# The first norm and modulation of a hybrid decoder block, rewritten: other products on TensorE, a quartered root, four differences on GpSimd

## The chip, the cores and the metric

The kernel runs on one core of a Trainium2 chip. The metric is the device time of one execution in microseconds (us). A kernel's time here is the median of several runs. Beside the timed runs, one execution was recorded by the hardware profiler; its span (first to last instruction) is a little shorter than its device time.

The engines are named as the profile names them: PE (TensorE, matrix products; PEld is its loading of the stationary operand), DVE (VectorE), ACT (ScalarE), POOL (GpSimd), SP (SyncE, which issues most transfers here).

## What is computed

One layer of a decoder block for 512 tokens of width 1024, all in float32. The part that matters here is the first line of it: the norm over each token, scaled and shifted by a vector that is computed from the condition `c`.

```python
mod = silu(c) @ ada_w + ada_b                       # 1024 x 6144
shift1, scale1, gate1, shift2, scale2, gate2 = split(mod, 6)
h = rmsnorm(x, norm1_g) * (1 + scale1) + shift1     # x: 512 x 1024
q, k, v, cb, cc, cu = split(h @ w_in, ...)          # 1024 x 2304
...                                                 # attention, short conv, output projection
x = x + gate1 * (merged @ w_out)
h2 = rmsnorm(x, norm2_g) * (1 + scale2) + shift2
x = x + gate2 * peer(h2, ...)                       # product-key experts, nearly all of the time
```

## The kernel before, in words

The activations lie transposed: `xT` holds the 1024 channels as 8 chunks of 128 partitions by 512 tokens. Matrix products that must keep float32's accuracy are made from two parts: `hi` is the operand rounded by ACT (`split`, L176), `lo` is what was cut off, a difference made by DVE (L177), and `mm3` (L200 to L202) adds three products of them in one accumulator.

The first stage goes so. ACT squares the 8 chunks of `xT` (L221), DVE adds them up one after the other (L223), and one product with a matrix of ones (`ss`, L253) sums over the partitions and puts the same sum on all of them, for 512 tokens. ACT takes the root (L241), DVE the reciprocal (L242), both over 128x512. In the meantime `silu(c)` is spread to all partitions as `cact` (`rows_of`, L156 to L160: DVE builds diagonal blocks `dg`, two products with ones turn them into rows).

Then the 8 chunks of `h` are made in the order 5, 6, 7, 0 to 4 (`ORDER`). The shift and scale of a chunk come from `ada_w` in one of two ways. For the chunks 5 to 7 (`NR` = 3), PE multiplies a broadcast column of `silu(c)` with 256 columns of `ada_w` (`ada_rows`, L272, eight products a chunk), which leaves shift and scale as rows on all partitions, and DVE picks the diagonal (`pick`, L290). For the other five, DVE multiplies a transposed 128x1024 block with `cact` and sums it up (`junk`, L213), once for the shift and once for the scale. After that `h` takes four operations a chunk: `f` = x times 1/rms (DVE, L295), scaled and shifted in place (ACT, L296), `hH` (ACT, L176) and `hL` (DVE, L177).

Four blocks of `w_in` (`FIRST`: 4, 5, 0, 1) are loaded between them and split into `hi` and `lo`; as each chunk of `h` is ready, PE runs the 12 products of that chunk into four accumulators `pj`. Weights, `ada_w` blocks and `dg` share five buffers (`LD` = 5, tag `ld`), so SP can issue a transfer only when the user of the buffer five places earlier is done.

Behind this come the angles for the rotary embedding (DVE L313 to L326, ACT `sinT` L324 and `cosT` L327), the norms and rotations of q and k (`q0`, `qk1`, `qk2`: ACT L353 and L355, PE `ssq` L357 and `rot` L368, DVE L363 to L372), and further blocks of `w_in` (`PLAN`: P2, P3 and so on). Each engine has one queue and works it off in order. A scheduler sets that order before the run, from costs of its own; it is fixed in the program.

## Time and profile before

| | us |
|---|---|
| median of 3 timed runs | 1447.48 (1445.46 to 1451.26) |
| the profiled execution, device time | 1445.51 |
| its span | 1443.6 |

How to read it: every row of the profile has a start or a count, a duration, the engine, the line (L177 is line 177 of the kernel before), the operation, `out<-in` by the program's names, and the shape. A product of two float32 operands stands as two MATMUL rows, one for each of its passes (four products of 128x2 are eight rows). Rows of one kind that follow each other are merged, with their count.

### The profile page before, as it was taken

How to read it: one execution, taken by the hardware profiler on the slowest of the kernel's cores; microseconds unless marked ns; L12 is line 12 of the kernel's file. 1: busy time of each engine (PE TensorE's matmuls, PEld its weight loads, DVE VectorE, ACT ScalarE, POOL GpSimd, SP SyncE). 2: the span in 40 equal slices, each digit the busy share in tenths (PEclk: the TensorE clock that was granted, in tenths of full speed). 3: DMA queues.
4: the chain of work that ended last, by engine and by line, in shares of the span. 5: the costliest groups of instructions: out<-in, count | busy, mean ns of one | idle time of the engine just before them, and what ended most of it. 6: DMA issues, size and time to landing. Idle time of an engine off the chain costs nothing.

```text
span 1443.6 us, 21238 instructions
## 1 busy us (share of the span) xinstructions
PE 1391.7 (96%) x7696; PEld 1222.1 (85%) x7696; DVE 1242.0 (86%) x2267; ACT 616.1 (43%) x1041; POOL 411.4 (29%) x292
## 2 busy tenths in 40 slices
PE   6999998999897999999999999999999999999998
PEld 4776776788897999999888888889999999889997
DVE  7778978799989999998668888888789988898964
ACT  4534646423633555464433434343343324333431
POOL 0000000000032330511034444446545546565400
PEclk9999999999998999999999999999999999999999
DMA  8645535222496997898999999999999999999843
GB/s 282 226 164 166 202 124 188 82 85 89 151 305 200 382 377 280 327 384 325 364 332 362 409 395 378 396 357 380 355 362 394 388 357 343 363 343 393 319 146 131
DMA packets 134377, 418.80 MB, mean 290 GB/s; under 512 B 12801, under 2 KB 39553, under 8 KB 132737
## 3 DMA queue, kind: packets, MB, share of 16 engines
q1 hardware_dynamic: 92800, 266.45, 51.1%
q0 software_dynamic: 41472, 151.01, 27.7%
q8 instruction: 60, 0.98, 0.3%
q14 instruction: 45, 0.36, 0.1%
HBM read 375.77 MB, written 41.62 MB: 289 GB/s over the span
## 4 chain that ended last, share of the span: by engine, by line
PE 63%; DVE 24%; DMA 5%; issue 5%; ACT 2%; POOL 1%; SPq 0%; DVEq 0%; ACTq 0%; POOLq 0%
PE o L997 11%; PE o L996 11%; PE o L998 11%; PE pa L200 6%; PE pa L202 6%; PE pa L201 6%; DVE lo L177 4%; DVE junk L213 2%; DVE B L946 2%; DVE junk L784 1%; PE py L200 1%; PE py L201 1%; DVE I L636 1%; PE py L202 1%; POOL row L776 1%
## 5 line engine op out<-in xcount | busy, mean ns | idle before, releaser
L176 ACT ACTIVATE hi<-raw 128x1024 fp32r<-128x1024 f32 x298 | 312.2, 1054 | 308.2 <-PE pa L201 71.7
L177 DVE TENSOR_TENSOR lo<-raw,hi 128x1024 fp32r<-128x1024 f32 x298 | 363.2, 1221 | 42.4 <-ACT hi L176 42.0
L202 PE MATMUL pa<-h2H,lo 128*128 128x352 f32 x1024 | 330.5, 323 | 8.2 <-DVE lo L177 8.2
L200 PE MATMUL pa<-h2H,hi 128*128 128x352 f32 x1024 | 332.9, 325 | 1.4 <-ACT sp L624 1.4
L201 PE MATMUL pa<-h2L,hi 128*128 128x352 f32 x1024 | 329.5, 322 | 0.0
L997 PE MATMUL o<-lo,wwh 128*128 128x512 f32 x768 | 299.2, 390 | 0.9 <-DVE lo L177 0.9
L996 PE MATMUL o<-hi,wwh 128*128 128x512 f32 x768 | 299.6, 390 | 0.0
L998 PE MATMUL o<-hi,wwl 128*128 128x512 f32 x768 | 298.8, 389 | 0.0
L776 POOL DMA_INDIRECT row<-in_uR,eG x128 | 187.4, 1464 | 319.5 <-PE o L998 181.8
L776 POOL DMA_INDIRECT row<-in_vL,eG x128 | 179.8, 1405 | 135.4 <-PE o L998 68.6
L784 DVE SCALAR_TENSOR_TENSOR junk<-row,h2N 128x1024 bf16<-128x1024 f32 x128 | 154.2, 1224 | 63.0 <-DMA row<-in_uR,eG 62.8
L202 PEld LDWEIGHTS pa<-h2H,lo 128*128 128x128 f32 x1024 | 193.2, 189 | 9.4 <-DVE lo L177 9.4
L200 PEld LDWEIGHTS pa<-h2H,hi 128*128 128x128 f32 x1024 | 192.7, 188 | 3.7 <-ACT sp L624 1.5
L201 PEld LDWEIGHTS pa<-h2L,hi 128*128 128x128 f32 x1024 | 193.1, 189 | 2.2
L912 DVE SCALAR_TENSOR_TENSOR ga<-row,av,ga 128x1024 f32<-128x1024 f32 x127 | 163.1, 1284 | 29.7 <-DMA row<-in_vL,eG 22.0
L776 POOL DMA_INDIRECT row<-in_uR,eH x32 | 44.0, 1376 | 493.2 <-DVE eq L695 402.9
L998 PEld LDWEIGHTS o<-hi,wwl 128*128 128x128 f32 x768 | 144.2, 188 | 30.3
L997 PEld LDWEIGHTS o<-lo,wwh 128*128 128x128 f32 x768 | 144.2, 188 | 29.3 <-DVE lo L177 1.5
L996 PEld LDWEIGHTS o<-hi,wwh 128*128 128x128 f32 x768 | 144.1, 188 | 28.3 <-issue 0.2
L176 ACT ACTIVATE wwh<-w 128x768 fp32r<-128x768 f32 x64 | 54.2, 846 | 164.0 <-DVE w L979 118.0
L978 ACT ACTIVATE w<-G 128x32 f32<-128x32 f32 x128 | 22.3, 221 | 190.4 <-DVE wwl L177 179.9
L177 DVE TENSOR_TENSOR wwl<-w,wwh 128x768 fp32r<-128x768 f32 x64 | 61.1, 955 | 9.8 <-ACT wwh L176 9.8
(265 smaller groups left out, 1852.0 us busy)
## 6 DMA issues: line engine op xcount, KB each, us to landing
raw<-in_uL SPq DMA_DIRECT2D x128, 512.0 KB
raw<-in_vL SPq DMA_DIRECT2D x128, 512.0 KB
Gd<-st SPq DMA_DIRECT2D x12, 2048.0 KB
G<-Gd SPq DMA_DIRECT2D x16, 1536.0 KB
ada<-in_ada SPq DMA_DIRECT2D x32, 512.0 KB
Ad<-sp SPq DMA_DIRECT2D x34, 352.0 KB
sp<-Ad SPq DMA_DIRECT2D x34, 352.0 KB
raw<-in_w_in SPq DMA_DIRECT2D x18, 512.0 KB
```

The source lines that it names most:

```text
L176: nc.scalar.activation(h, f, AF.Copy)
L177: nc.vector.tensor_sub(l, f, h.bitcast(F32))
L200: nc.tensor.matmul(ps, wh(k), rh(k), start=(k == k0), stop=False)
L201: nc.tensor.matmul(ps, wh(k), rl(k), start=False, stop=False)
L202: mark[0] = nc.tensor.matmul(ps, wl(k), rh(k), start=False, stop=(k == k1))
L213: nc.vector.scalar_tensor_tensor(junk, raw, 1.0, cact, op0=OP.mult, op1=OP.mult, accum_out=mod[:, b:b + 1])
L776: d = nc.gpsimd.indirect_dma_start(out=t, out_offset=None, in_=tab, in_offset=bass.IndirectOffsetOnAxis(ap=e, axis=0))
L784: return nc.vector.scalar_tensor_tensor(junk, t, 1.0, h, op0=OP.mult, op1=OP.mult, accum_out=a)
L912: nc.vector.scalar_tensor_tensor(ga, t, av[:, k:k + 1], ga, op0=OP.mult, op1=OP.add)
L996: nc.tensor.matmul(o, wh[:, cs], vh[:, hs], start=(j == 0), stop=False)
L997: nc.tensor.matmul(o, wh[:, cs], vl[:, hs], start=False, stop=False)
L998: last = nc.tensor.matmul(o, wl[:, cs], vh[:, hs], start=False, stop=(j == NJ - 1))
```

## The change

It rewrites the first stage and leaves the rest of the kernel's text alone.

- `silu(c)` as rows: eight products of a broadcast column with the identity take the place of the diagonal blocks on DVE. `rows_of` is used once more near the end of the kernel, for `gate2`.
- Sum of squares: DVE adds only pairs (four additions for seven). Each pair goes to PE at once, as four products with 32 columns of ones; each handles 128 tokens and writes to its own 32 partitions (`grouped`). So 1/rms is worked out on 128x128 (`grouped_root`), and four products with a broadcast column of the identity spread it to 128x512 in PSUM (`spread`, tile `rr`).
- Chunks go in the order 0 to 7. The shift of chunks 0 to 3 (`NR` = 4) comes from PE: eight products of a 128x128 block of `ada_w` with one column of `silu(c)` (`shift`). All eight scales and the other four shifts come from DVE (`junk`): 12 such operations for 10.
- `h` takes three operations a chunk, those that the second norm has already (`modulated`, L227 to L231): `f` with scale and 1/rms at once, `hH` with the shift, `hL` with the shift.
- The `lo` parts of the four first weight blocks go to GpSimd (`by`).
- The eight blocks of `ada_w` for the scales are loaded to two buffers of their own (tag `ada`), beside the five.

```diff
--- before.py
+++ after.py
@@ -41,8 +41,7 @@
 LD = 5
 AHEAD = 7
 LAST = 8
-NR = 3
-WHEN = (-1, 0, 2, 3)
+NR = 4
 PACE = (1.75, 4.2)
 
 
@@ -152,11 +151,11 @@
 
     def rows_of(dst, cols):
 
-        dg = ld.tile([P, 8, P], F32, tag="ld", bufs=LD, name="dg")
-        nc.vector.tensor_mul(dg, ident[:, None, :].to_broadcast([P, 8, P]), cols[:, :, None].to_broadcast([P, 8, P]))
         for k in range(2):
             ps = psa.tile([P, 512], F32, tag="a", name="ro")
-            nc.tensor.matmul(ps, ones, dg[:, 4 * k:4 * k + 4, :], start=True, stop=True)
+            for i in range(4):
+                nc.tensor.matmul(ps[:, i * P:(i + 1) * P], cols[:, 4 * k + i:4 * k + i + 1].to_broadcast([P, P]), ident,
+                                 start=True, stop=True)
             nc.scalar.activation(dst[:, k * 512:(k + 1) * 512], ps, AF.Copy)
 
     a1, a1_s = pool("a1")
@@ -172,26 +171,26 @@
             tc.add_manual_dep(ins.ins, mark.ins.name, mybir.DependencyInfo(
                 mybir.DependencyClass.Sync, mybir.DependencyReason.DATA), reason="pace")
 
-    def split(h, l, f):
+    def split(h, l, f, by=nc.vector):
         nc.scalar.activation(h, f, AF.Copy)
-        nc.vector.tensor_sub(l, f, h.bitcast(F32))
+        by.tensor_sub(l, f, h.bitcast(F32))
 
     def load(src):
         raw = ld.tile([P, D], F32, tag="ld", bufs=LD, name="raw")
         nc.sync.dma_start(raw, src)
         return raw
 
-    def parts(src):
+    def parts(src, by=nc.vector):
 
         raw = load(src)
         h = hl.tile([P, D], F32R, tag="h", bufs=4, name="hi")
         l = hl.tile([P, D], F32R, tag="l", bufs=4, name="lo")
-        split(h, l, raw)
+        split(h, l, raw, by)
         return h, l
 
-    def weights_of(src):
-
-        h, l = parts(src.rearrange("p a b -> p (a b)"))
+    def weights_of(src, by=nc.vector):
+
+        h, l = parts(src.rearrange("p a b -> p (a b)"), by)
         return (lambda k: h[:, k * P:(k + 1) * P]), (lambda k: l[:, k * P:(k + 1) * P])
 
     def mm3(ps, w, rh, rl, ks=range(DC), k0=0, k1=DC - 1):
@@ -236,73 +235,73 @@
         nc.scalar.activation(q, b, AF.Square)
         nc.tensor.matmul(ps, ones if w is None else w, q, start=(i == 0), stop=(i == n - 1))
 
+    def grouped(ps, q, first, last):
+
+        for c in range(NCH):
+            end = nc.tensor.matmul(ps[32 * c:32 * c + 32, 0:P], ones[:, 0:32], q[:, c * P:(c + 1) * P], start=first,
+                                   stop=last)
+        return end
+
+    def grouped_root(ps, n):
+        r = cp.tile([P, P], F32, tag="r", name="r", bufs=1)
+        nc.scalar.activation(r, ps[:, 0:P], AF.Sqrt, scale=1.0 / n, bias=eps)
+        nc.vector.reciprocal(r, r)
+        return r
+
+    def spread(r):
+
+        ps = psa.tile([P, 512], F32, tag="a", name="rr")
+        for c in range(NCH):
+            nc.tensor.matmul(ps[:, c * P:(c + 1) * P], ident[:, 32 * c:32 * c + 1].to_broadcast([P, P]), r,
+                             start=True, stop=True)
+        return ps
+
     def rstd(ps, n):
         r = tmp("rstd")
         nc.scalar.activation(r, ps, AF.Sqrt, scale=1.0 / n, bias=eps)
         nc.vector.reciprocal(r, r)
         return r
 
-    modv = mod.rearrange("p (a k) -> p a k", a=6)
-    adabv = S("ada_b").rearrange("p (a k) -> p a k", a=6)
-
 
     ps = bank("ss1")
-    sq = None
-    for k in range(DC):
-        sq = squared(xT[:, k, :], sq)
-    nc.tensor.matmul(ps, ones, sq, start=True, stop=True)
-    r1 = rstd(ps, D)
+    for k in range(0, DC, 2):
+        grouped(ps, squared(xT[:, k + 1, :], squared(xT[:, k, :])), k == 0, k == DC - 2)
     hH = a1.tile([P, DC, T], F32R, tag="hH", name="hH")
     hL = a1.tile([P, DC, T], F32R, tag="hL", name="hL")
     hh, hlo = (lambda k: hH[:, k, :]), (lambda k: hL[:, k, :])
     FIRST = (4, 5, 0, 1)
     pj, wj = {}, {}
-
-    psr = [None]
-
-    def ada_rows(r):
-
-        if r % 2 == 0:
-            psr[0] = psa.tile([P, 2, 2, P], F32, tag="a", name="psr")
-        ps = psr[0][:, r % 2]
-        for n in range(2):
-            w = load(p["adaR"][r, n].rearrange("p a b -> p (a b)"))
-            for i in range(4):
-                kb = 4 * n + i
-                nc.tensor.matmul(ps, ccol[:, kb:kb + 1].to_broadcast([P, P]), w[:, i * 256:(i + 1) * 256],
-                                 start=(kb == 0), stop=(kb == DC - 1))
-        return ps
-
-    ORDER = (*range(DC - NR, DC), *range(DC - NR))
-    def some_weights(m):
-        for b, w in zip(FIRST, WHEN):
-            if w == m:
-                wj[b] = weights_of(p["w_in"][b])
-
-    some_weights(-1)
-    for m, k in enumerate(ORDER):
-        if k < DC - NR:
-            ada((k, 8 + k))
-        else:
-            ps = ada_rows(m)
-            for q in range(2):
-                pick = rt.tile([P, P], F32, tag="pick", name="pick", bufs=1)
-                nc.vector.scalar_tensor_tensor(pick, ps[:, q, :], 1.0, ident, op0=OP.mult, op1=OP.mult,
-                                               accum_out=modv[:, q, k:k + 1])
-        nc.vector.tensor_add(modv[:, 0:2, k], modv[:, 0:2, k], adabv[:, 0:2, k])
+    shift = bank("shift")
+    r1 = None
+    for k in range(DC):
+        for b in (8 + k,) if k < NR else (8 + k, k):
+            if b == k:
+                raw = load(p["ada"][b])
+            else:
+                raw = a1.tile([P, D], F32, tag="ada", bufs=2, name="ada")
+                nc.sync.dma_start(raw, p["ada"][b])
+            junk = rt.tile([P, D], BF16, name="junk", **R2)
+            nc.vector.scalar_tensor_tensor(junk, raw, 1.0, cact, op0=OP.mult, op1=OP.mult, accum_out=mod[:, b:b + 1])
+        if k < NR:
+            w = load(p["adaR"][k].rearrange("p a b -> p (a b)"))
+            for i in range(DC):
+                nc.tensor.matmul(shift[:, k:k + 1], w[:, i * P:(i + 1) * P], ccol[:, i:i + 1], start=(i == 0),
+                                 stop=(i == DC - 1))
+        if k == 0:
+            r1 = spread(grouped_root(ps, D))
+        if k < len(FIRST):
+            wj[FIRST[k]] = weights_of(p["w_in"][FIRST[k]], nc.gpsimd)
+        nc.vector.tensor_add(mod[:, k:k + 1], shift[:, k:k + 1] if k < NR else mod[:, k:k + 1], S("ada_b", k))
+        nc.vector.tensor_add(mod[:, 8 + k:9 + k], mod[:, 8 + k:9 + k], S("ada_b", 8 + k))
         nc.vector.scalar_tensor_tensor(s1[:, k:k + 1], mod[:, 8 + k:9 + k], 1.0, S("n1g", k), op0=OP.add, op1=OP.mult)
-        f = tmp("f")
-        nc.vector.tensor_mul(f, xT[:, k, :], r1)
-        nc.scalar.activation(f, f, AF.Identity, scale=s1[:, k:k + 1], bias=mod[:, k:k + 1])
-        split(hH[:, k, :], hL[:, k, :], f)
-        some_weights(m)
-        if m == 4:
+        modulated(hH[:, k, :], hL[:, k, :], xT[:, k, :], r1, s1[:, k:k + 1], mod[:, k:k + 1])
+        if k == 4:
             nc.sync.dma_start(cs2, p["cst"][:, KEEP:])
     for b in FIRST:
         pj[b] = bank("pj")
-    for k in ORDER:
+    for k in range(DC):
         for b in FIRST:
-            mm3(pj[b], wj[b], hh, hlo, [k], ORDER[0], ORDER[-1])
+            mm3(pj[b], wj[b], hh, hlo, [k])
 
 
     pos = tmp("pos").bitcast(I32)
```

What the scheduler makes of it is shown at three places; from the first rotations on, the order on every engine is the same as before, apart from the second use of `rows_of`. Line numbers are those of each program: the lines of `split` and `mm3` stand one lower in the changed kernel.

First DVE, from the last sum of squares to the first `hL`. Before:

```order
L223 TENSOR_TENSOR sq<-sq 128x512 x7
L177 TENSOR_TENSOR lo<-raw,hi 128x1024
L242 RECIPROCAL rstd<-rstd 128x512
L290 SCALAR_TENSOR_TENSOR pick,mod<-psr,cst 128x128
L295 TENSOR_TENSOR f<-xT,rstd 128x512
L290 SCALAR_TENSOR_TENSOR pick,mod<-psr,cst 128x128
L177 TENSOR_TENSOR lo<-raw,hi 128x1024
```

The same place now (`shift` is PE's product, `rr` the spread 1/rms, `s` the scale):

```order
L222 TENSOR_TENSOR sq<-sq 128x512 x4
L284 SCALAR_TENSOR_TENSOR junk,mod<-ada,cact 128x1024
L295 TENSOR_TENSOR mod<-mod,sm 128x1
L296 SCALAR_TENSOR_TENSOR s_103<-mod,sm 128x1
L294 TENSOR_TENSOR mod<-shift,sm 128x1
L248 RECIPROCAL r<-r 128x128
L228 SCALAR_TENSOR_TENSOR f<-xT,s_103,rr 128x512
L284 SCALAR_TENSOR_TENSOR junk,mod<-ada,cact 128x1024
L230 SCALAR_TENSOR_TENSOR hL<-f,mod,hH 128x512
```

The reciprocal now stands behind the addition that takes PE's first shift, and a `junk` stands between `f` and `hL`.

Then PE, from the first shift on (`pj` are the accumulators of the first four blocks of `w_in`). Now:

```order
L288 MATMUL shift<-ccol,raw 128x1 x8
L255 MATMUL rr<-r,cst 128x128 x4
L199 MATMUL pj<-hH,hi 128x512
L288 MATMUL shift<-ccol,raw 128x1 x8
L200 MATMUL pj<-hL,hi 128x512
L201 MATMUL pj<-hH,lo 128x512
L199 MATMUL pj<-hH,hi 128x512
L200 MATMUL pj<-hL,hi 128x512
L199 MATMUL pj<-hH,hi 128x512
L201 MATMUL pj<-hH,lo 128x512
L199 MATMUL pj<-hH,hi 128x512
L288 MATMUL shift<-ccol,raw 128x1 x8
```

Where all 24 products of `ada_rows` stood ahead of the first `pj` product, the second shift stands behind one of them and the third behind eight. The fourth follows after 15 more:

```order
L201 MATMUL pj<-hH,lo 128x512 x2
L199 MATMUL pj<-hH,hi 128x512
L200 MATMUL pj<-hL,hi 128x512
L288 MATMUL shift<-ccol,raw 128x1 x8
L201 MATMUL pj<-hH,lo 128x512
```

The second of the two products in the first row takes the `lo` of the third weight block, which GpSimd makes; so the fourth shift now stands behind GpSimd's third difference.

Last ACT, behind the stage (`hi` are parts of the next blocks of `w_in`, `rstd` the root for k's norm). Before:

```order
L324 ACT_TABLE_LOAD
L324 ACTIVATE sinT<-f 128x512
L327 ACTIVATE cosT<-f_431 128x512
L461 ACTIVATE vT<-pj 128x512
L353 ACTIVATE qn<-pj,sm 128x512
L355 ACTIVATE sq<-pj 128x512
L353 ACTIVATE qn<-pj,sm 128x512
L355 ACTIVATE sq<-pj 128x512
L236 ACTIVATE sq<-pj 128x512
L176 ACTIVATE hi<-raw 128x1024 x2
L241 ACT_TABLE_LOAD
L241 ACTIVATE rstd<-ss,eps 128x512
```

Now:

```order
L352 ACTIVATE qn<-pj,sm 128x512
L354 ACTIVATE sq<-pj 128x512
L352 ACTIVATE qn<-pj,sm 128x512
L354 ACTIVATE sq<-pj 128x512
L235 ACTIVATE sq<-pj 128x512
L175 ACTIVATE hi<-raw 128x1024
L323 ACT_TABLE_LOAD
L323 ACTIVATE sinT<-f 128x512
L326 ACTIVATE cosT<-f_451 128x512
L261 ACT_TABLE_LOAD
L261 ACTIVATE rstd<-ss,eps 128x512
```

Sine and cosine, with their table, moved from ahead of the five operations on q and k to behind them; `vT` and two more `hi` stand just ahead of these rows.

## Rows read from the trace of the kernel before

**Rows 1.** The page's busy times of each engine.

```profile
PE 1391.7 (96%) x7696; PEld 1222.1 (85%) x7696; DVE 1242.0 (86%) x2267; ACT 616.1 (43%) x1041; POOL 411.4 (29%) x292
```

**Rows 2.** Stretches: length, busy us of PE, PEld, DVE, ACT, POOL, granted clock, DMA, GB/s.

```profile
35.00:40.00 5.00, 3.57 (x16) 2.66 (x15) 5.00 (x12) 2.88 (x5) 0.00 (x0) 1.00 1.02 385
...
60.00:65.00 5.00, 5.00 (x16) 3.31 (x16) 4.25 (x3) 3.33 (x4) 0.00 (x0) 0.75 0.62 210
65.00:70.00 5.00, 5.00 (x24) 3.75 (x23) 4.07 (x5) 1.54 (x2) 0.00 (x0) 1.00 0.37 111
```

**Rows 3.** Timeline, first norm: start us, us, engine, line, operation, out<-in, shape.

```profile
9.16 4.67 DVE L223 TENSOR_TENSOR sq<-sq 128x512 f32<-128x512 f32 x6 [1.85 <-ACT sq L221]
...
13.88 2.08 PE L253 MATMUL ss<-sq,ones 128*128 128x512 f32 x2 [3.88 <-DVE sq L223]
...
16.71 3.35 DVE L242 RECIPROCAL rstd<-rstd 128x512 f32<-128x512 f32 x1 [1.60 <-ACT rstd L241]
...
25.32 0.69 DVE L177 TENSOR_TENSOR hL<-f,hH 128x512 fp32r<-128x512 f32 x1
```

**Rows 4.** Groups on DVE, 0 to 60 us: busy us, mean ns, idle before.

```profile
L213 DVE SCALAR_TENSOR_TENSOR junk<-raw,cact 128x1024 bf16<-128x1024 f32 x10 | 12.1, 1220 | 0.0
L177 DVE TENSOR_TENSOR lo<-raw,hi 128x1024 fp32r<-128x1024 f32 x6 | 7.3, 1223 | 6.1 <-ACT hi L176 6.0
...
L290 DVE SCALAR_TENSOR_TENSOR pick<-psr,cst 128x128 f32<-128x128 f32 x6 | 1.7, 287 | 0.5 <-PE psr L272 0.5
...
L150 DVE RECIPROCAL csig<-csig 128x8 f32<-128x8 f32 x1 | 0.2, 203 | 0.0
```

**Rows 5.** Chain of waits: float32 products of 2 and of 128 columns.

```profile
76.47 0.79 PE ssq L357 x8
...
120.74 1.11 PE po L425 x8
```

**Rows 6.** The second norm's modulation by line: ns min/median/max, starts, shapes.

```profile
L229 DVE SCALAR_TENSOR_TENSOR f<-xT,s,rstd x8: 747/748/752, 237.8 to 246.7; 128x512 f32<-128x512 f32 x8
L231 DVE SCALAR_TENSOR_TENSOR fL<-f,mod,fH x8: 747/748/752, 240.1 to 248.4; 128x512 fp32r<-128x512 f32 x8
```

**Rows 7.** Timeline, from the last `hL` to the second rotation.

```profile
50.85 0.69 DVE L177 TENSOR_TENSOR hL<-f,hH 128x512 fp32r<-128x512 f32 x1
...
52.64 0.63 ACT L324 ACTIVATE sinT<-f 128x512 f32<-128x512 f32 x1 [0.77 <-DVE f L323]
...
57.41 2.04 ACT L176 ACTIVATE hi<-raw 128x1024 fp32r<-128x1024 f32 x2
...
59.47 1.28 ACT L241 ACT_TABLE_LOAD   x1
60.76 0.69 ACT L241 ACTIVATE rstd<-ss,eps 128x512 f32<-128x512 f32 x1
...
66.60 0.74 DVE L363 SCALAR_TENSOR_TENSOR qn<-pj,sm,rstd 128x512 f32<-128x512 f32 x1
...
67.39 1.13 PE L368 MATMUL rot<-qn,cs 128*128 128x512 f32 x2
...
67.96 0.79 PE L200 MATMUL pj<-hH,hi 128*128 128x512 f32 x1
```

**Rows 8.** A fill of 128x1 on POOL and on DVE, mean ns.

```profile
L1124 POOL MEMSET const-float32-1.0<- 128x1 f32 x1 | 0.1, 105 | 0.0
...
L133 DVE MEMSET eps<- 128x1 f32 x1 | 0.1, 59 | 0.0
```

**Rows 9.** Timeline of PE: two-column products at 56 us and what follows them.

```profile
56.06 2.12 PE L357 MATMUL ssq<-cs,sq 128*128 128x2 f32 x16 [0.84 <-ACT sq L355]
...
58.58 0.90 PE L200 MATMUL pj<-hH,hi 128*128 128x512 f32 x1
...
59.70 1.91 PE L368 MATMUL rot<-qn,cs 128*128 128x512 f32 x2
```

**Rows 10.** Chain of waits near the end: the second use of `rows_of`.

```profile
1420.80 1.72 PE ro L159 x4
```

More of the change, by code (lines that the diff above doesn't have):

```diff
@@ L1104, in layout @@
         "cst": constants(),
[L1105 to L1107 removed]
+        "adaR": rows(f["ada_w"][0][:, 0:NR * P]),
         "ada": np.ascontiguousarray(f["ada_w"][0].T.reshape(48, P, D)),
```

3 lines of the change are left out of this document (removed).

## Prediction

> **What bounds the kernel now.** Over the whole run PE is busy 96% of the span, DVE 86% [rows 1], but the change lies in the first 50 us, so I read that stretch by itself. The table of 5 us stretches shows who is full there: at 35 to 40 us DVE is busy 5.00 of 5.00 and PE 3.57; at 65 to 70 us it is PE that is full and DVE at 4.07 [rows 2]. So the first stage ends when DVE ends it, and behind it PE sets the pace. Microseconds won or lost up to the first blocks behind the stage are handed on to the end, since the order behind them does not change. I therefore follow three times: when the first `f` starts on DVE, when the last `hL` ends, and when the second rotation is past and PE runs full.
>
> Before, the last sum of squares ends at 9.16 + 4.67 = 13.83, the sum over partitions at 13.88 + 2.08 = 15.96, the reciprocal at 16.71 + 3.35 = 20.06, and the first `hL` at 26.01 [rows 3]. The last `hL` ends at 50.85 + 0.69 = 51.54, and the first product behind the second rotation starts at 67.96 [rows 7].
>
> **First term: up to the first `f`.** ACT still makes eight squares and two copies, and the last addition of a pair ends about where the last of seven ended, 13.8. What follows is now a chain over PE and DVE.
>
> Four products of 32 columns of ones with 128 tokens are eight passes. The nearest row is the eight passes of `po` (128 columns) in 1.11, or 0.14 each [rows 5]. In rows 3 PE took 2.08 for two passes of 512, where the pair of `rot` passes at 67.39 took 1.13 with its tail [rows 7]: PE is at its lower level (1.2 of 2.4 GHz) at 14 us. So the price is 1.1 to 2.2: 14.9 to 16.0.
>
> The reciprocal stands behind the addition that takes the first shift. That shift is 16 passes of one column; the nearest row is eight passes of two columns in 0.79, 0.10 each [rows 5]. So 1.6, or 3.2 at the lower level: 16.5 to 19.2.
>
> The reciprocal of 128x8 took 0.20 [rows 4] and that of 128x512 3.35 [rows 3], that is 0.00625 a column; 128 columns come to 0.95: 17.5 to 20.2. Eight passes of `rr` are another 1.1 to 2.2: the first `f` starts at 18.7 to 22.4. The middle is 20.5. I take it, since rows 3 show PE at the lower level at the start of this chain and it can rise within it.
>
> **Second term: from the first `f` to the last `hL`.** DVE's work, start to start. Eleven `junk` at 1.22 [rows 4] are 13.4. Eight `f` and eight `hL` in the form of the second norm take 0.75 each [rows 6]; neighbours overlap by nearly 0.1, so 16 at 0.66 are 10.6. Twenty-one additions and scales on one column, at 0.08, are 1.7. Together 25.7.
>
> To this come waits that the order makes, for a queue that is worked off in order:
> - The second shift stands on PE behind the first `pj` product, which needs `hH`. That is there 0.66 + 0.7 behind the start of `f`; 0.2 for the product and 1.6 for the shift make 3.3. DVE asks at 0.66 + 1.22 + 0.66 = 2.5 and waits 0.8.
> - The third shift stands behind the next `hH` and two products: by the same steps 3.7 behind the second `f`, asked for at 2.6; wait 1.1.
> - The third `hL` follows its `f` directly and waits for ACT: 0.7.
> - The fourth shift stands behind a product with GpSimd's third difference. ACT's `hi` for it follows the third `hH`, so GpSimd starts 0.66 + 0.7 + 1.0 = 2.4 behind the third `f`. Then GpSimd's own time, three products (0.7) and the shift (1.6): 4.7 plus GpSimd's time. DVE asks at 4.4. The wait is 0.3 plus GpSimd's time.
> - The fourth `hH` needs that shift, and `hL` waits for it: 0.7.
>
> GpSimd's time has no row. From below, DVE's own time for this difference is 1.22 [rows 4]. From above, the slowest elementwise rate in the trace is DVE's reciprocal, 0.0065 a column [rows 3]: 6.7 for 1024 columns. A small fill took 105 ns on POOL and 59 ns on DVE [rows 8], a ratio of 1.8, and I take 1.22 x 1.8 = 2.2, near the lower end; it is a guess from a small operation. The four waits other than the fourth come to 3.3, the fourth to 2.5 (1.5 to 7.0).
>
> The Trainium skill's page GPSIMD Engine Reference (section Elementwise, side-by-side cycle accounting) measures 4497 ns for such an operation on 2048 columns; by it the time would be near 2.25, an estimate, and the sum the same.
>
> So 25.7 + 5.8 = 31.5 lie between the first `f` and the last `hL`: 20.5 + 31.5 = 52.0, with 50.2 to 53.9 from the first term. Before it was 51.54. The first two terms nearly cancel: **+0.5**.
>
> What is taken off DVE is real: four `lo` at 1.22, six `pick` at 0.29 [rows 4], three additions at the 0.69 of `hL` [rows 3], `dg` as long as a `lo` and 2.4 of the reciprocal are 12.3, against 2.4 for two more `junk`. It does not reach the end, because the shifts that PE now returns one by one, each in front of other work of DVE, cost 5.8 in waits, and because chunks 5 to 7 no longer go ahead without a `junk`.
>
> **Third term: behind the stage.** Before, 67.96 - 51.54 = 16.4 pass from the last `hL` to the first product behind the second rotation [rows 7]. Sine and cosine then lay under the last products. Now ACT has them behind the work on q and k. Counted from the last `hL`: the first accumulators and the first `hi` at about 1.4, that `hi` 1.0, `vT` 0.6, the second `hi` 1.0 (with 0.2 of waits), five operations of 0.57, the third `hi` 1.0, a table 1.28, sine and cosine 1.2, a table 1.28, the root 0.7: 12.5. Reciprocal 3.35, `cosT` times q 0.66, `qn` 0.74, the rotation's two passes 0.9: 18.2. PE waits for it, as before it waited for `qn` at 66.60. That is **+1.8**.
>
> **Fourth term: the end.** The four passes of `ro` on the chain near the end took 1.72 [rows 10]. Now they are 16 of 128 columns, at 0.107 (a quarter of 0.43) to 0.14 [rows 5]: 1.7 to 2.2, so **+0.3**. `dg` there is taken from DVE at a time when PE sets the pace, and counts nothing.
>
> At nothing I set the transfers: the same 16 blocks of `ada_w` are loaded, with two more buffers, so they start earlier. SP's queue is held by each scale block until a `junk` two chunks back is done, and what stands behind it (a shift block or a block of `w_in`) waits with it; if a block came late by that, each `junk` waiting on it would cost what it is late. GpSimd has no other work until long after.
>
> The sum is 0.5 + 1.8 + 0.3 = +2.6. On the profiled execution's own 1445.51 that is 1448.1; the median before is 1447.48, and I give the forecast against it: **1450.1**. 0.5% of the median, 7.2, is about what a measurement of this kernel can tell from no change. Chance 0.47, with 1446 to 1455 as this case's own range (first term -1.8 to +1.9, GpSimd -1.0 to +4.5).
>
> **Rivals.**
>
> *PE stays at its lower level through the first four chunks.* The trace shows how it can: two-column products from 56.06 on, and then a 512-column product takes 0.90 and a rotation 1.91 [rows 9], and the granted clock of 60 to 65 us is 0.75 [rows 2]. Three pieces of 16 one-column passes now lie among sparse `pj` products. The first term goes to its upper end (+1.9), each of the three shifts takes 1.6 more, and 15 products between the third and the fourth take 0.2 more each: 1.9 + 4.8 + 3.0 = 9.7 on top, some of it under GpSimd's time; I give it 8, 1458. Against it: PE stays at the higher level at 35 to 40 us, with 1.4 of 5 us idle. It decides if `pj` rows of 0.6 and more last until the fourth shift. Chance 0.26.
>
> *GpSimd's differences hold DVE up.* While GpSimd reads two tiles, DVE's operations on two tiles in SBUF would wait: 4 x 2.2. The first lies under the reciprocal, the third under the wait for the fourth shift; of the second and fourth some 3 to 4 would be paid, 1453.5. No row of before has elementwise work on POOL, so none speaks for or against. This is a rule of the Trainium skill's page SBUF — State Buffer (section Who interferes with whom): a DVE instruction with two inputs in SBUF contends with a GpSimd instruction that reads SBUF, and whichever starts second is blocked for the other's whole length. Chance 0.15.
>
> *The other side: the shifts come back in time, and DVE's saving shows.* With no wait the last `hL` ends at 18.7 + 25.7 = 44.4, or 7.1 earlier; the third term gives 1.8 back and the end 0.3: -5, 1442.5. It decides where the second shift is back 2.5 behind the start of `f`, that is, where 16 passes take under 0.9, against 1.6 by rows 5, and the fourth is not held by GpSimd, though its place is fixed behind that product. Chance 0.12.
>
> **How the numbers follow.** Faster by over 7.2 (under 1440.3) is the far part of the last rival: 0.04. Slower by over 7.2 (above 1454.7) takes nine tenths of the first rival, a third of the second and the tail of the likeliest: 0.33. Between them 0.63. The range of 1443 to 1460 leaves out half of the last rival below (0.06) and some 0.12 above, the part of the first rival in which nothing is hidden.
>
> **What would show it.** In the changed kernel's profile: the last addition at 13.8, `rr` done by 18.5 to 22, the first `f` behind it; DVE waiting for PE ahead of the second, third and fourth shift, most ahead of the fourth; the last `hL` at 50 to 54; sine some 9 behind it and PE idle ahead of the second rotation; one GpSimd difference near 2.2. Wrong would be: `junk` rows that wait for transfers, GpSimd's first difference starting long after its `hi`, `pj` rows at twice 0.39, or DVE without gaps from 20 us on.

## The result and the profile after

The changed kernel takes 1455.77 us (median of 9 runs, 1450.99 to 1460.66) against 1447.48 of the kernel before beside it (9 runs, 1442.37 to 1451.87): a ratio of 1.0066, 95% interval 1.0045 to 1.0088, or 8.3 us more. The forecast was 2.6 more. The profiled execution took 1460.66 with a span of 1458.7 and was the longest of the nine; a second profile, taken with the experiments in an execution of 1454.77, has nearly the same rows up to the last `hL`.

The page of the changed kernel has PE busy for 96% of the span and DVE for 85%, against 96% and 86% [rows 1]. Nothing shows there; the stage has to be read by itself. First DVE's timeline of the changed kernel, from the last addition of squares to the last `hL` (start, us, engine, line, operation, in brackets idle before it and who ended that; answers to [rows 3] and the first row of [rows 7]):

```profile
12.01 0.69 DVE L222 TENSOR_TENSOR sq<-sq 128x512 f32<-128x512 f32 x1 [0.34 <-ACT sq L220]
...
16.95 0.16 DVE L294 TENSOR_TENSOR mod<-shift,sm 128x1 f32<-128x1 f32 x1 [2.72 <-PE shift L288]
17.03 0.94 DVE L248 RECIPROCAL r<-r 128x128 f32<-128x128 f32 x1
20.13 0.75 DVE L228 SCALAR_TENSOR_TENSOR f<-xT,s,rr 128x512 f32<-128x512 f32 x1 [2.17 <-PE rr L255]
...
25.72 0.16 DVE L294 TENSOR_TENSOR mod<-shift,sm 128x1 f32<-128x1 f32 x1 [3.04 <-PE shift L288]
...
32.62 0.16 DVE L294 TENSOR_TENSOR mod<-shift,sm 128x1 f32<-128x1 f32 x1 [3.82 <-PE shift L288]
...
35.09 1.22 DVE L284 SCALAR_TENSOR_TENSOR junk<-ada,cact 128x1024 bf16<-128x1024 f32 x1
...
36.35 2.20 DVE L295 TENSOR_TENSOR mod<-mod,sm 128x1 f32<-128x1 f32 x1
...
41.32 0.16 DVE L294 TENSOR_TENSOR mod<-shift,sm 128x1 f32<-128x1 f32 x1 [1.79 <-PE shift L288]
...
44.20 2.22 DVE L295 TENSOR_TENSOR mod<-mod,sm 128x1 f32<-128x1 f32 x1
...
59.75 1.62 DVE L230 SCALAR_TENSOR_TENSOR hL<-f,mod,hH 128x512 fp32r<-128x512 f32 x2
```

The first `f` starts at 20.13, where the forecast put it (20.5). The last `hL` ends at 59.75 + 1.62 = 61.37, 9.4 later than forecast and 9.8 later than before [rows 7]. Between the two lie 41.24. Of these, 8.65 are the three waits for `shift`, 1.58 two waits for `hH` (0.79 each), and 4.10 two additions of a single column that took 2.20 and 2.22 where their like takes 0.16. What is left, 26.9, is the work.

PE's timeline shows why the shifts are late:

```profile
12.76 0.65 PE L241 MATMUL ss<-sq,ones 128*32 128x128 f32 x8 [0.38 <-DVE sq L222]
13.34 3.57 PE L288 MATMUL shift<-ccol,raw 128*128 128x1 f32 x16
18.02 2.07 PE L255 MATMUL rr<-r,cst 128*128 128x128 f32 x8 [1.11 <-DVE r L248]
...
22.28 3.41 PE L288 MATMUL shift<-ccol,raw 128*128 128x1 f32 x16
...
26.55 0.63 PE L199 MATMUL pj<-hH,hi 128*128 128x512 f32 x1
...
29.18 3.41 PE L288 MATMUL shift<-ccol,raw 128*128 128x1 f32 x16
...
39.40 1.89 PE L288 MATMUL shift<-ccol,raw 128*128 128x1 f32 x16
...
47.49 0.39 PE L199 MATMUL pj<-hH,hi 128*128 128x512 f32 x1
```

Sixteen one-column passes take 3.41 to 3.57 three times and 1.89 the fourth time. `pj` products take 0.63 in between, against 0.39 later: by these rows PE runs at its lower level (1.2 GHz) up to about 37 us. The clock column of the stretch table reads 1.00 there in this execution and 0.50 in the second, whose rows are nearly the same; the last section shows both. Behind the fourth group `pj` rows are at 0.63 again until 43 us; in the second profile they are not. GpSimd's four differences are:

```profile
15.16 2.34 POOL L176 TENSOR_TENSOR lo<-raw,hi 128x1024 fp32r<-128x1024 f32 x1 [14.71 <-ACT hi L175]
22.66 2.35 POOL L176 TENSOR_TENSOR lo<-raw,hi 128x1024 fp32r<-128x1024 f32 x1 [5.16 <-ACT hi L175]
35.41 3.12 POOL L176 TENSOR_TENSOR lo<-raw,hi 128x1024 fp32r<-128x1024 f32 x1 [10.41 <-ACT hi L175]
43.26 3.14 POOL L176 TENSOR_TENSOR lo<-raw,hi 128x1024 fp32r<-128x1024 f32 x1 [4.73 <-ACT hi L175]
```

One takes 2.34. The third starts at 35.41 while DVE's `junk` runs until about 36.2, and ends 2.3 behind that, at 38.53; DVE's one-column addition, begun at 36.35, ends at 38.55. In each case the one that began second waited for the other's end. The two differences at 15.16 and 22.66 met DVE waiting or in the reciprocal, and cost nothing.

Behind the stage, the timeline of the changed kernel (PE, ACT and DVE, in order of time; answers to [rows 7] and [rows 9]):

```profile
66.81 2.52 PE L356 MATMUL ssq<-cs,sq 128*128 128x2 f32 x16 [1.43 <-ACT sq L354]
69.19 2.05 PE L236 MATMUL ss<-sq,cs 128*128 128x512 f32 x2
```

```profile
70.56 0.63 ACT L323 ACTIVATE sinT<-f 128x512 f32<-128x512 f32 x1
...
73.75 3.35 DVE L262 RECIPROCAL rstd<-rstd 128x512 f32<-128x512 f32 x1 [3.10 <-ACT rstd L261]
79.56 0.69 DVE L370 TENSOR_TENSOR qn<-qn,cosT 128x512 f32<-128x512 f32 x1 [2.46 <-PE rot L367]
...
81.53 0.80 PE L199 MATMUL pj<-hH,hi 128*128 128x512 f32 x1
```

Sine comes 9.2 behind the last `hL`, as forecast (9). From the last `hL` to the first product behind the second rotation 20.2 pass (16.4 before, 18.2 forecast): up to 75 us PE is again at its lower level, and the first rotation, for which DVE waits 2.46, stands in PE's queue behind products of which eight take 0.63 instead of 0.39. The stretch table (columns as in [rows 2]) has it:

```profile
70.00:75.00 5.00, 5.00 (x12) 3.43 (x11) 1.90 (x2) 4.61 (x6) 0.00 (x0) 0.50 0.43 138
```

So this first product starts at 81.53 instead of 67.96, 13.6 later; in the second profile, where DVE waits 0.73 for that rotation, at 80.22, 12.3 later.

### The profile page after: what moved, and what is told of

Its sections match the earlier page's. It is cut to its first block, busy times and chain, and to the rows that moved or that the text cites. A ratio compares the mean times of both kernels' runs of the same rounds, so it can differ in the third digit from the quotient of the medians.

```text
span 1458.7 us, 21382 instructions
## 1 busy us (share of the span) xinstructions
PE 1406.5 (96%) x7774; PEld 1236.9 (85%) x7774; DVE 1237.9 (85%) x2258; ACT 609.6 (42%) x1033; POOL 423.7 (29%) x296
## 4 chain that ended last, share of the span: by engine, by line
PE 65%; DVE 23%; DMA 5%; issue 4%; ACT 2%; POOL 1%; SPq 0%; DVEq 0%; POOLq 0%; ACTq 0%
PE o L996 11%; PE o L997 11%; PE o L995 11%; PE pa L201 6%; PE pa L199 6%; PE pa L200 6%; DVE lo L176 4%; DVE B L945 2%; DVE junk L783 1%; DMA row<-in_vL,eG 1%; PE pj L199 1%; PE pj L201 1%; PE pj L200 1%; PE py L199 1%; PE py L200 1%
## 5 line engine op out<-in xcount | busy, mean ns | idle before, releaser
L176 DVE TENSOR_TENSOR lo<-raw,hi 128x1024 fp32r<-128x1024 f32 x294 | 357.5, 1217 | 40.7 <-ACT hi L175 40.2
```

Source lines behind the costliest of these rows:

```text
L176: by.tensor_sub(l, f, h.bitcast(F32))
```

## The experiments

The theory after the first comparison: two costs make up the loss, PE's lower level (late shifts) and the mutual hold-up of GpSimd and DVE. Rivals: the loss comes from elsewhere (order, transfers, the work behind the stage). All marks below are from one profile each; ratios are to the kernel before on the same chip, with 95% intervals. Waits for `shift` are counted from the first `f` on. "Held" is what operations of DVE took beyond their usual time while GpSimd worked; "mark" is the first product behind the second rotation.

| kernel | first `f` | waits for `shift` | held | last `hL` ends | mark | ratio |
|---|---|---|---|---|---|---|
| before | 20.82 | none | 0 | 51.54 | 67.96 | |
| changed | 20.13 | 8.65 | 4.10 | 61.37 | 81.53 | 1.0066 (1.0045 to 1.0088) |
| changed, again | 20.63 | 8.61 | 4.06 | 61.80 | 80.22 | 1.0070 (1.0054 to 1.0086) |
| `lo` on DVE | 20.91 | 3.50 | 0 | 54.17 | 72.80 | 1.0061 (1.0039 to 1.0083) |
| 128 columns | 16.00 | 0 | 6.70 | 49.00 | 68.98 | 1.0000 (0.9986 to 1.0015) |
| no shift products | 19.18 | none | 6.46 | 55.07 | 75.02 | 1.0034 (1.0018 to 1.0050) |
| that, `lo` on DVE | 19.19 | none | 0 | 51.47 | 71.38 | 1.0013 (0.9993 to 1.0033) |
| one column, other order | 19.91 | 3.52 | 6.13 | 58.22 | 76.67 | 1.0055 (1.0040 to 1.0070) |
| 128 columns, changed order | 18.72 | 3.12 | 4.02 | 55.16 | 75.65 | 1.0053 (1.0033 to 1.0072) |
| 128 columns, `lo` on DVE | 18.57 | 0.47 | 0 | 48.99 | 69.08 | 1.0015 (1.0000 to 1.0029) |
| before, `lo` on GpSimd | 21.96 | none | 3.9 | 54.22 | 75.32 | 1.0047 (1.0028 to 1.0066) |
| before, wide q sums | 20.16 | none | 0 | 52.16 | 68.13 | 0.9992 (0.9973 to 1.0012) |
| 128 columns, wide q sums | 17.90 | 0 | 6.27 | 50.33 | 68.85 | 0.9988 (0.9974 to 1.0002) |
| that, `lo` on DVE | 18.89 | 0.46 | 0 | 49.31 | 68.15 | 1.0010 (0.9994 to 1.0026) |

From the mark to the end the fourteen profiled executions take 1371.7 to 1379.3, in no order that follows the edits. So a difference of a few us at the mark is shown by the rows and not by the times.

**`lo` on DVE again.**

```diff
-            wj[FIRST[k]] = weights_of(p["w_in"][FIRST[k]], nc.gpsimd)
+            wj[FIRST[k]] = weights_of(p["w_in"][FIRST[k]])
```

> The changed kernel with one thing undone: the four `lo` differences of the first weights are made on DVE again, not on GpSimd. Theory (two costs: GpSimd's differences and DVE's operations on two SBUF tiles shut each other out, and PE at its lower level returns the shifts late): the two one-column additions of 2.20 and 2.22 us go back to 0.16, which gives 4.1; four `lo` at 1.22 come back on DVE, the first two under waits that are there anyway, so 1 to 2.5 of them are paid. PE's waits stay. The last `hL` ends at 58 to 60 instead of 61.4, and the median falls by 2 to 4, to 1452 to 1454. Rival (the hold-ups lie under the waits for PE, and only PE's level counts): the last `hL` stays at 61 to 63 and the time at 1455 to 1458.

No operation is held, and the last `hL` ends 7.2 earlier, more than expected, because the waits shrink too. The edit changed more than the engine of `lo`: the scheduler put the second shift on PE ahead of the first `pj` product, where it had stood behind it, and a `junk` ahead of the third and the fourth addition that waits. And PE is at its higher level for the third and fourth group, though these too have one column. On DVE, then on PE:

```profile
24.11 0.16 DVE L294 TENSOR_TENSOR mod<-shift,sm 128x1 f32<-128x1 f32 x1 [0.65 <-PE shift L288]
...
29.88 0.16 DVE L294 TENSOR_TENSOR mod<-shift,sm 128x1 f32<-128x1 f32 x1 [1.63 <-PE shift L288]
```

```profile
28.00 1.84 PE L288 MATMUL shift<-ccol,raw 128*128 128x1 f32 x16
29.70 0.47 PE L200 MATMUL pj<-hL,hi 128*128 128x512 f32 x1
```

The median, 1452.63, is in the expected place, but the ratio can't be told from that of the changed kernel. The rows are on the theory's side where hold-ups are concerned; how much of the 7.2 is theirs can't be read from this run, and that the time follows is not shown. The run also says that one-column products do not always keep PE down: ten `pj` products in a row came ahead of the third group, PE rose during them (0.63, then 0.39), and it stayed up behind both later groups.

**128 columns in place of one.** Each product of a shift takes its column of `ccol` 128 times; the first of 128 equal results is read.

```diff
-                nc.tensor.matmul(shift[:, k:k + 1], w[:, i * P:(i + 1) * P], ccol[:, i:i + 1], start=(i == 0),
+                nc.tensor.matmul(shift[:, k * P:(k + 1) * P], w[:, i * P:(i + 1) * P], ccol[:, i:i + 1].to_broadcast([P, P]), start=(i == 0),
...
```

> The changed kernel, but each product of a shift takes the column of `ccol` 128 times (128 equal columns, of which the first is read) instead of once; everything else is the same. Theory (one-column products let the granted clock fall): with 128 columns PE comes to its higher level before the second or third shift; the second and third group of 16 passes take about 1.9 instead of 3.4, `pj` rows 0.39 instead of 0.63 there, DVE's waits for `shift` fall from 8.65 to 3 to 5, the last `hL` ends near 56, and the median is near 1451. Rival (the level is low in this stretch because PE has gaps and starts cold, whatever the width): the groups take 3.4 to 3.8 each, `pj` rows stay at 0.63, the last `hL` ends at 61 to 63, and the median is at 1455 to 1458.

Better than either expectation: level with the kernel before, the whole loss gone, though GpSimd held DVE up for 6.7, more than in the changed kernel. On PE:

```profile
12.77 2.05 PE L288 MATMUL shift<-ccol,raw 128*128 128x128 f32 x16
...
23.80 3.29 PE L288 MATMUL shift<-ccol,raw 128*128 128x128 f32 x16
```

Two things speak against reading it as width alone. The third group is at the lower level again (3.29), and DVE does not wait for it. And DVE's queue is no longer the same, presumably since the scheduler counts a wide product as longer: the reciprocal now stands ahead of the addition that takes the first shift, and each later addition of a shift behind the `f` of its chunk instead of ahead of it (`f` does not need the shift, only `hH` and `hL` do). Two runs below tell these apart.

**The products for shifts undone, with `lo` on GpSimd and on DVE.** All eight shifts come from a `junk`:

```diff
+NS = 0
...
-        for b in (8 + k,) if k < NR else (8 + k, k):
+        for b in (8 + k,) if k < NS else (8 + k, k):
...
-        if k < NR:
+        if k < NS:
             w = load(p["adaR"][k].rearrange("p a b -> p (a b)"))
```

> The changed kernel with the four products for shifts undone: all eight shifts come from a `junk` on DVE, as chunks 4 to 7 do in the changed kernel; `lo` stays on GpSimd. Theory: DVE's waits for `shift` (8.65) go, four `junk` at 1.22 (4.9) come, of which the first lies under the wait for `rr`; the hold-ups by GpSimd stay, and since DVE is fuller GpSimd's 4 x 2.34 may cost it up to 2 more. The last `hL` ends at 55 to 58 instead of 61.4, and the median falls by 3 to 6. Rival (the loss comes from the order of the chunks, late transfers or the work behind the stage): the last `hL` stays at 60 or later and the time within 2 of 1455.8.

> The changed kernel with both undone: all eight shifts from a `junk` on DVE, and the four `lo` on DVE. What is left of the change: squares summed in groups, the root on quarters, the three-operation form of `f`, chunks in order, and `cact` by broadcast columns. Theory (these two costs are the whole loss of the stage): DVE runs without long gaps from the first `f` on; the last `hL` ends at 50 to 54, and the median is 1445 to 1449, level with the kernel before within 3. If the two costs simply add, its gain over the changed kernel is the sum of what the two undone alone gain. Rival (something else in what is left is dear): the last `hL` ends after 56 and the median stays above 1452.

Both as the theory has it. The first ends the stage at 55.07 with three additions held, 6.46 in all; the second at 51.47 with no wait and nothing held, 0.07 before the kernel before. It shows that the rest of the change (grouped squares, root on quarters, the form of `f`, chunks in order) costs nothing in the stage, taken together. The two gains don't add (6.3 and 7.2 alone, 9.9 together): without waits DVE is full, and its own 32.3 of work bound the stage. In both, PE is at its lower level in this stage without any thin product. In the first, the granted clock is 0.50 from 20 to 35 us, PE being idle for a third of the time:

```profile
20.00:25.00 5.00, 2.87 (x5) 1.46 (x5) 5.00 (x6) 1.63 (x2) 3.29 (x1) 0.50 0.76 266
```

In the second, the same stretch reads 1.00, but its `pj` rows take 0.63 up to 33 us as well:

```profile
20.00:25.00 5.00, 3.79 (x7) 2.27 (x8) 5.00 (x9) 2.69 (x3) 0.00 (x0) 1.00 0.80 292
```

```profile
23.24 0.63 PE L201 MATMUL pj<-hL,hi 128*128 128x512 f32 x1
```

So thin products are not needed for the lower level; full-width products with gaps between them leave PE there too.

**The changed kernel again, and width and order apart.** In the version with one column the order was set by two dependencies (on the reciprocal, on `f`); in the one with 128 columns DVE's queue was held in the changed kernel's order through the first four chunks (`rec[0]` is the reciprocal, `add` the addition that takes the shift, `two` and `one` the addition and scale of s1).

```diff
...
+        now = nc.vector.scalar_tensor_tensor(f, xT[:, k, :], s1[:, k:k + 1], r1, op0=OP.mult, op1=OP.mult)
+        add = nc.vector.tensor_add(mod[:, k:k + 1], shift[:, k:k + 1] if k < NR else mod[:, k:k + 1], S("ada_b", k))
+        if k < NR:
+            after(add, now if k else rec[0])
...
```

```diff
...
+        if k == 0:
+            r1 = spread(grouped_root(ps, D))
+            after(rec[0], add)
+        if k in (1, 2):
+            after(two if k == 1 else one, add)
...
```

> The changed kernel once more, as it is, beside the others of this set and with a second profile of it. Both theories below: its ratio to the kernel before is 1.0045 to 1.009 as in the first comparison. If PE's lower level in the first 45 us is a property of the program and not of one execution, the groups of 16 one-column passes again take 3.4 in at least two of the last three, and the last `hL` ends after 58; if it is a matter of the single execution, it can end at 52 to 57.

> The changed kernel with one-column products as they are, but DVE's queue in the order in which the version with 128 columns has it: the reciprocal ahead of the addition that takes the first shift, and the addition that takes a shift behind `f` of its chunk instead of ahead of it. Since the version with 128 columns differed in this too, this run and the next tell width and order apart. Theory width (the thin products keep PE at its lower level): groups still take 3.4, `pj` 0.63; the order alone takes some 1 from the front and up to 0.75 from each wait; the last `hL` ends at 56 to 60, the median is 1 to 4 below the changed kernel's. Rival order (what mattered is what stands behind the waiting addition): the last `hL` ends at 49 to 53 and the median is level with the kernel before within 3.

> The changed kernel with 128 columns in each product of a shift, and DVE's queue held in the order of the changed kernel through the first four chunks (on PE the second shift then stands ahead of the first `pj` product, not behind it). Theory width: PE comes to its higher level, the groups take 1.9 to 2.3, DVE's waits for `shift` are under 4 in all, the last `hL` ends at 50 to 54, and the median is level with the kernel before within 3. Rival order: PE may be at the higher level, but DVE waits for each shift with `f` behind it; the last `hL` ends at 56 or later, the median stays 6 or more above the kernel before.

The changed kernel repeats itself: groups of 3.57, 3.40, 3.41 and 1.84, held 4.06, the last `hL` at 61.80. Neither width nor order alone does it: the last `hL` comes 3.2 earlier by order, 6.2 by width, and both medians stay 8 above the kernel before. So the theory of width is half right, and so is its rival, the theory of order. PE of the version with one column, then of the one with 128:

```profile
14.38 3.58 PE L290 MATMUL shift<-ccol,raw 128*128 128x1 f32 x16
17.81 2.06 PE L257 MATMUL rr<-r,cst 128*128 128x128 f32 x8
```

```profile
12.69 3.52 PE L293 MATMUL shift<-ccol,raw 128*128 128x128 f32 x16
17.52 1.16 PE L258 MATMUL rr<-r,cst 128*128 128x128 f32 x8 [1.31 <-DVE r L250]
...
26.01 3.58 PE L293 MATMUL shift<-ccol,raw 128*128 128x128 f32 x16
```

Both groups start at the lower level. Behind one-column passes `rr` is at that level still, 2.06 to 2.08 in all four profiles of such kernels; behind 128-column passes that began at the lower level it takes 1.06 to 1.70, in all four of those. So width is what brings PE up here, in either order. But it falls again where PE is idle half of 20 to 25 us (third group 3.58), and in the changed order DVE pays for that:

```profile
29.62 0.16 DVE L297 TENSOR_TENSOR mod<-shift,sm 128x1 f32<-128x1 f32 x1 [3.12 <-PE shift L293]
```

In the other order a group at the same level (3.29, above) lay under work of DVE that stands ahead of the addition.

**128 columns and `lo` on DVE.** The two edits together.

> The changed kernel with 128 columns in each product of a shift, and the four `lo` on DVE. Against the version with 128 columns alone (last `hL` at 49.0): theory two costs says that its three held one-column operations (2.32, 2.25, 2.26) and the lengthened `junk` (1.57) go back, 6.7 in all, against four `lo` at 1.22, of which one lies under a wait; the last `hL` ends at 46 to 49 and the median is 0 to 3 below that version's. Rival (only the width counted, GpSimd's work is free): four `lo` more on a full DVE, the last `hL` ends at 52 to 54 and the median is 2 to 4 above.

The last `hL` ends at 48.99, level with 49.00, with nothing held. The first `f` came 2.6 later than in the version with 128 columns alone. There PE had come to its higher level ahead of the first shift (2.05, above, against 3.78 here), which looks like a matter of that execution: the profile of the same version with wide q sums, below, has 3.77 and its first `f` at 17.90. From the first `f` on, 30.4 pass against 33.0: the hold-ups of 6.7 were worth 2.6 more than three `lo` on DVE (the fourth lies ahead of `f`). The median that should have been up to 3 below isn't: 1.0015 against 1.0000, with intervals that overlap. So with 128 columns no loss in time by GpSimd's work is shown, here or in the pair with wide q sums (0.9988 against 1.0010).

**The kernel before, with `lo` on GpSimd alone.**

```diff
...
-                wj[b] = weights_of(p["w_in"][b])
+                wj[b] = weights_of(p["w_in"][b], nc.gpsimd)
```

> The kernel before with one part of the change alone: the `lo` differences of the first four weights on GpSimd. Nothing else is touched; the scheduler may place things anew. Theory (GpSimd's difference and a DVE operation on two SBUF tiles shut each other out): DVE is full in this stage, so each difference that starts in it holds DVE up by some 2.1, as in the changed kernel; three or four of them, 6 to 8, against four `lo` of 1.15 to 1.22 taken off DVE, 4.7. The last `hL` ends at 52.5 to 55 instead of 51.5 and the median is 1 to 4 above. Rival (GpSimd's work is free, what it takes off DVE is won): no held operation, the last `hL` ends at 46 to 48 and the median is 2 to 4 below.

This single edit costs 6.8 us (1.0047), more than the 1 to 4 expected. The timeline of POOL and DVE shows both cases of the rule:

```profile
18.09 2.34 POOL L177 TENSOR_TENSOR lo<-raw,hi 128x1024 fp32r<-128x1024 f32 x1 [1.44 <-ACT hi L176]
...
28.69 2.37 POOL L177 TENSOR_TENSOR lo<-raw,hi 128x1024 fp32r<-128x1024 f32 x1 [8.26 <-ACT hi L176]
```

```profile
17.11 3.35 DVE L242 RECIPROCAL rstd<-rstd 128x512 f32<-128x512 f32 x1 [2.89 <-ACT rstd L241]
...
29.13 3.02 DVE L213 SCALAR_TENSOR_TENSOR junk<-raw,cact 128x1024 bf16<-128x1024 f32 x1 [0.50 <-DMA raw<-in_ada]
```

The reciprocal has one input; it and GpSimd's second difference ran side by side at 3.35 and 2.34, as each does alone. The `junk` has two inputs in SBUF and took 3.02 instead of 1.22. The last `hL` comes 2.7 later, as expected; another 4.7 are lost behind it (21.1 to the mark against 16.4). There the scheduler placed sine behind `vT`, as in the changed kernel, and PE is at its lower level behind q's sums (`ss` takes 2.06, six `pj` 0.62 or 0.63); what each of the two costs was not separated. This edit thus carries part of the third term as well, and 1.0047 is not the price of the hold-ups alone.

**Wider sums of q's squares**, on the kernel before and on the two versions with 128 columns: 32 columns of `blk` instead of two.

```diff
-            nc.tensor.matmul(ssq[:, c, b:b + 5:4], q[:, c * P:(c + 1) * P], blk[:, 0:65:64], start=True, stop=True)
+            nc.tensor.matmul(ssq[:, c, b, :], q[:, c * P:(c + 1) * P], blk[:, 48:80], start=True, stop=True)
...
```

> The kernel before, with the products for the sums of q's squares taken 32 columns wide (16 equal columns for each head, of which one is read) instead of two; the first norm is untouched. It carries the finding on thin products to another place: before, PE falls to its lower level behind the two-column products at 56 us, and the product and rotation behind them take 0.90, 1.91 and 1.41. Theory (thin products let PE's clock fall): PE stays at the higher level, these rows become 0.4 to 0.8 and 1.0, and the first product behind the second rotation starts 1 to 2.5 earlier than 67.96; the median is 0 to 3 below, too little to be sure of by times alone, so the rows decide. Rival (PE falls there because it waits for ACT): the rows stay as they are, and the mark stays at 67 to 69.

> The version with 128 columns in the products of the shifts (level with the kernel before), with the 32-column sums of q's squares added. Theory: the last `hL` again at 49 to 52 (it also shows whether the first `f` at 16.0 was one execution's), PE at the higher level behind it, the first product behind the second rotation 1 to 3 earlier than 68.98, and the median 0 to 4 below the kernel before. Rival (the width of those products changes nothing): products of 0.63 behind the sums, the mark at 68 to 70, the median level with the kernel before.

> The same with the four `lo` on DVE: 128 columns for the shifts, 32 for the sums of q's squares, nothing on GpSimd. Theory: the last `hL` at 47 to 50, products at 0.4 behind the sums, the mark 1 to 3 earlier than 69.08, the median 0 to 4 below the kernel before, and level with the version that has `lo` on GpSimd within 2. Rival: the mark stays at 68 to 70 and the median 0 to 4 above the kernel before.

On the kernel before, PE's timeline now reads, where [rows 9] had 0.90 and 1.91:

```profile
57.00 2.15 PE L357 MATMUL ssq<-cs,sq 128*128 128x32 f32 x16 [0.59 <-ACT sq L355]
...
59.52 0.79 PE L200 MATMUL pj<-hH,hi 128*128 128x512 f32 x1
...
60.38 1.02 PE L368 MATMUL rot<-qn,cs 128*128 128x512 f32 x2
```

PE stays at the higher level (granted clock 1.00 in every stretch from 50 to 75 us; the `pj` behind the 0.79 takes 0.39), sixteen times as many columns take 2.15 instead of 2.12, and from the last `hL` to the mark 16.0 pass instead of 16.4: less than expected; that ACT and DVE set the pace there was not tested.

On the two versions with 128 columns the theory failed. PE falls behind the wide sums too, with `lo` on GpSimd (first fence) and with `lo` on DVE (second):

```profile
55.76 2.15 PE L356 MATMUL ssq<-cs,sq 128*128 128x32 f32 x16 [1.43 <-ACT sq L354]
...
59.99 0.63 PE L200 MATMUL pj<-hL,hi 128*128 128x512 f32 x1
```

```profile
55.13 2.15 PE L356 MATMUL ssq<-cs,sq 128*128 128x32 f32 x16 [1.43 <-ACT sq L354]
...
58.56 0.63 PE L200 MATMUL pj<-hL,hi 128*128 128x512 f32 x1
```

The marks, 68.85 and 68.15, lie where the rival put them. The distance from the last `hL` to the mark falls from 20.0 and 20.1 to 18.5 and 18.8, but with `lo` on GpSimd all of that lies ahead of the sums: from their start to the mark 13.04 pass with two columns and 13.09 with 32, and two columns gave 12.99 in the second profile of the changed kernel. PE waits 1.43 for ACT ahead of the sums in both versions, and 0.59 in the kernel before with wide sums. So the rival that PE falls there because it waits for ACT is not excluded, and one profile in which the level holds does not show that the width held it.

The version with both widths is 1.7 below the kernel before by its ratio, 0.9988, but its interval reaches 1.0002: no version is shown to beat the kernel before.

## Why the prediction was off

The median of 1455.77 lies in the stated 1443 to 1460, but not in the 1446 to 1455 of the likeliest case, and a loss of more than 7.2 had been given 0.33. That the forecast is off by 5.7 us and not by 11 is partly luck: at the mark 13.6 are lost where 2.3 were forecast, and the time shows 8.3.

**First term** (first `f` at 20.5): right, 20.13 and 20.63, but by luck, since errors in its parts cancel. The last addition of squares ended at 12.70, not 13.8; the eight passes of `ss` took 0.65, not 1.1 to 2.2; the first shift 3.57, beyond the upper end of 3.2; the reciprocal 0.94 (0.95); `rr` 2.07 of 1.1 to 2.2.

**Second term** (last `hL` at 52.0): this step failed, by 9.4. The work was well sized, 26.9 for 25.7. The waits were not: 5.8 in all was forecast, 10.2 came. The second and third shift, put at waits of 0.8 and 1.1, cost 3.04 and 3.82, mostly since 16 passes took 3.41 and not 1.6. The fourth, for which most was set aside (2.5), cost 1.79. And 4.1 of hold-ups stood in no term. So two rivals came true at once, not the likeliest case; the prediction had set each by itself and none for both together. *PE at its lower level* named the mechanism, the price (1.6 more for each shift; 1.8 measured) and the rows that decide it, and 1458 lies in the range of the runs; `pj` rows of 0.63 lasted to 37 us, just short of the fourth shift at 39.4. *GpSimd's differences hold DVE up* put 3 to 4 on it; 4.1 came, at the third and fourth difference instead of the second and fourth. The argument against the first rival, that PE holds its level at 35 to 40 us with 1.4 of 5 idle, was taken from a stretch in which PE was at that level already, and did not carry over to one that begins at the lower level.

What that accounting missed is that the waits also hang on the order of DVE's queue. In the changed order the addition that takes a shift stands ahead of `f`, which doesn't need it. With another order alone the waits for `shift` fall from 8.65 to 3.52, but the hold-ups rise to 6.13 and the last `hL` gains only 3.2; with width and order both the waits are gone, and with them the loss. In the changed kernel the hold-ups also take back most of what moving `lo` to GpSimd had taken off DVE, four times 1.22.

The price of 2.2 for a difference on GpSimd, guessed from two fills, was near: 2.34 where nothing holds it. By the Trainium skill's page GPSIMD Engine Reference (section Elementwise, side-by-side cycle accounting) an estimate of 2.25 followed; the rows agree within 4%. Its page SBUF — State Buffer (section Who interferes with whom) says that a DVE instruction with two inputs in SBUF and a GpSimd instruction that reads SBUF lock each other out for a whole instruction, and that DVE with at most one such input, outside its two-port modes, doesn't. The 3.02 of `junk` and the 3.35 of the reciprocal agree with both.

**Third term** (18.2 behind the stage): 20.2 and 18.4 in the two profiles of the changed kernel. The later sine came as described, and the second profile agrees within 0.2. The other 2.0 of the first profile is PE's lower level behind q's sums, which [rows 9] had shown already and the sum left out: it lasted longer in that execution, and DVE waited 2.46 for the first rotation instead of 0.73. What brings PE down there stays open; two columns instead of 32 are not shown to be the cause.

**Fourth term**: `ro` near the end is 1.95 on PE, within 1.7 to 2.2, and the transfers cost nothing: no `junk` of the stage waits for one.

```profile
1435.66 1.95 PE L157 MATMUL ro<-cst,mod 128*128 128x128 f32 x16
```

Together: +9.8 and +3.7 at the mark, 13.6, of which the time shows 8.3 (9.9 in the repetition). Whether the rest is given back later isn't shown; what follows the mark varies by more than that from one execution to the next.

## What to carry to other kernels

A product of one column is cheap only in columns: sixteen passes of 128 columns took hardly longer than sixteen of one (3.3 to 3.8 against 3.4 to 3.6 at the lower level, 1.95 against 1.84 at the higher), and where both began at the lower level the wide ones brought PE up and the thin ones didn't, in four profiles of each. Behind q's sums the same step from two columns to 32 did not keep PE up in two of three profiles, so look at the rows each time. Widening also moved DVE's operations, since the scheduler set another order: compare the order of the queues before giving the credit to the edit. An operation on GpSimd is not free because GpSimd is idle: ask what DVE does meanwhile, and place it where DVE waits or works with one input in SBUF. In a queue worked off in order, put the operation that waits for another engine behind all that doesn't need it.

## What the hardware showed that was not expected

- The lock between GpSimd and DVE takes even the smallest operation: an addition of 128x1 took 2.20 instead of 0.16, and from the first `f` on the eight profiles with GpSimd's differences have 21 held operations, 19 of which end with GpSimd's instruction, within 0.11; the other two are `junk`, which ended 1.1 behind it. The same kind of addition with its first input in PSUM (16.95 in the first timeline) took 0.16 in the middle of GpSimd's 15.16 to 17.50.
- Four products of 32 columns of ones, on four quarters of the output, must overlap, by their time: eight passes took 0.65 at the lower level and 0.43 at the higher, where eight full ones (`rr`) took 2.07 and 1.16.
- The granted clock in the stretch table is not always that of the rows. In the first profile of the changed kernel it reads 1.00 from 15 to 40 us, while rows there have twice their usual length; in the second profile, with the same rows, it reads 0.50 from 15 to 35. The rows are the safer guide. The first profile, then the second:

```profile
25.00:30.00 5.00, 4.87 (x16) 3.66 (x15) 3.01 (x8) 0.72 (x1) 0.01 (x1) 1.00 0.69 225
```

```profile
25.00:30.00 5.00, 4.87 (x16) 3.66 (x16) 3.01 (x8) 0.72 (x1) 0.51 (x1) 0.50 0.76 246
```

- The same holds for the two versions without shift products: the column reads 0.50 from 20 to 35 us in one and 1.00 in the other, and in both the `pj` rows take 0.63 until 33 to 36 us.
